# Seven-product blocks with additive weight sums, the first sum made by an accumulating DMA

## The chip, the cores and the metric

The kernel runs on one core of a Trainium2 chip. The metric is the device time of one execution in microseconds; the median of three runs of the kernel before is 1709.31 us (1709.23 to 1712.28). TensorE (PE) multiplies, VectorE (DVE) and ScalarE (ACT) work elementwise, GpSimd (POOL) and SyncE (SP) here mostly issue transfers; the program's DMAs run on 16 DMA engines.

## The reference

One decoder block on 256 tokens of width 2048, in float32: a SwiGLU FFN at half weight, a mixer of two head groups, a second FFN, and a final norm. The change touches the two FFNs alone.

```python
def swiglu_ffn(x, w_gate, w_up, w_down):
    return (jax.nn.silu(x @ w_gate) * (x @ w_up)) @ w_down
...
x = x + 0.5 * swiglu_ffn(rms_norm(x, ffn1_norm), ffn1_w_gate, ffn1_w_up, ffn1_w_down)
...
x = x + 0.5 * swiglu_ffn(rms_norm(x, ffn2_norm), ffn2_w_gate, ffn2_w_up, ffn2_w_down)
return rms_norm(x, final_norm)
```

The gate and up weights are 2048 x 5632, the down weights 5632 x 2048.

## The kernel before

**Units and splits.** Weights come in units of 512 x 512 (1 MB), as tiles `raw_...` of 128 partitions by 4 x 512. For accuracy every operand is taken as a high part and a low part: ACT casts the unit to its high part `hi` in two halves, VectorE subtracts to get the low part `lo`, and a product of a unit with 128 tokens is 12 matmuls of 128x512: eight with the high part, four with the low part. `parts_of` (line 180) does the split, `multiply` (line 231) the matmuls. Three sets of `hi` and `lo` are in use inside an FFN, so the splitting may run three units ahead of TensorE.

**A block of seven products.** `seven` (line 396) computes two token halves by two column groups of 512 for two of the row units with seven unit products in place of eight (Strassen's scheme in Winograd's form), and adds the other row units (`xs`) in the usual way. With four row units, as for gate and up, that is 7 x 12 + 4 x 24 = 180 matmuls. It uses four PSUM banks `a`, `c`, `e`, `d`. In the code's numbering, product 0 (p0) is w11, product 4 (p4) w12 - w11, product 5 (p5) w22 less that, product 6 (p6) w22 - w12, product 3 (p3) w21 less p5's operand, and products 2 and 1 are w22 and w21 by themselves. The differences are made on VectorE in the tiles of w11 and w12. p4 is copied out of bank `c` (`s5`) and added later; a product that serves two quadrants is copied out by ACT (`snap`). The stationary sides (`sf`) are sums of the normalised tokens, made once per FFN, or once per group of hidden units, by `seven_of` (line 360). Names in the trace carry these numbers: `lo_u1_2_p4` is the low part for p4 of block 2 of the first FFN's up projection, `x01` the first unit taken in the usual way.

**Order and queues.** Each FFN has five column steps `s`; each runs a gate block and an up block, and after steps 0, 2 and 4 the down projection `down`, with one block of its own and some plain units. That makes 13 blocks per FFN, 26 in all. All loads stand in one queue on SP, in the order of the program; each waits for its buffer. There are three `raw` buffers, and two `kept` ones for w11 and w12 of a block, which live through most of it: w12's is free after product 6's split, w11's after product 3's. The first block of the first FFN is special: its w11 is loaded and split ahead of it (`ready`). Within an engine instructions run in the order that the scheduler of the build gave them; the flag `order` pins a few.

Of the kernel before, what the change touches and what calls it, by code (L numbers as in the profile page):

```python
# [13 lines left out]
AF = mybir.ActivationFunctionType  # L14
ALU = mybir.AluOpType
AX = mybir.AxisListType

P = 128
# [6 lines left out]
CW = 512  # L25
NC_D = D // CW
UK = 4
# [22 lines left out]
def hybrid_block(ctx: ExitStack, tc: tile.TileContext, a: dict, out: bass.AP):  # L50
    nc = tc.nc
    Engine.pinned = False
    dve, act, pe = (Engine(tc, e) for e in (nc.vector, nc.scalar, nc.tensor))
# [105 lines left out]
    def load(src, name, pieces=((0, UK),), loaded=None, kept=False):  # L159
        if kept:  # L160
            raw = extra[1].tile([P, UK, CW], F32, tag="kept", name=f"raw_{name}", bufs=2)
        else:
            raw = raws.tile([P, UK, CW], F32, tag="raw", name=f"raw_{name}")
        for i, e in pieces:
            nc.sync.dma_start(raw[:, i:e, :], src[i * P : e * P].rearrange("(j p) c -> p j c", p=P))
            if loaded:
                loaded(i)
        return raw

    def splits_of(name):  # L170
        pool, bufs = splits, 2
        if extra:
            turn_of["split"] += 1
            if turn_of["split"] % 3 == 0:
                pool, bufs = extra[0], 1
        hi = pool.tile([P, UK, CW], F32R, tag="hi", name=f"hi_{name}", bufs=bufs)
        lo = pool.tile([P, UK, CW], F32R, tag="lo", name=f"lo_{name}", bufs=bufs)
        return hi, lo, [(hi[:, j, :], lo[:, j, :]) for j in range(UK)]
# [181 lines left out]
    def seven_of(sf, x0, x1, v, spare, parts, steps=None):  # L360

        a11, a12, a21, a22 = v[0, 0], v[0, 1], v[1, 0], v[1, 1]
        parts = iter(parts)

        def split(i, q):
            hi, lo = next(parts)
            act.copy(hi, q)
            dve.tensor_tensor(lo, q, f32(hi), op=ALU.subtract)  # L370
            sf[i] = [(hi[:, j, :], lo[:, j, :]) for j in range(UK)]

        sf.update({0: stationary(x0, 0), 1: stationary(x1, 0), 3: stationary(x1, 1)})
        dve.tensor_tensor(spare, a21, a22, op=ALU.add)
        split(4, spare)

        def adds():
            dve.tensor_tensor(a21, a11, a21, op=ALU.subtract)
            dve.tensor_tensor(a11, spare, a11, op=ALU.subtract)

        def rest():
            if steps is None:
                adds()
            split(5, a11)
            split(6, a21)
            dve.tensor_tensor(a12, a12, a11, op=ALU.subtract)
            split(2, a12)

        if steps is not None:
            steps.extend((adds, rest))  # L390
        return rest
# [1 line left out]
    def quad(tile):  # L393
        return tile.rearrange("p (j c) -> p j c", j=UK)

    def seven(w, rows, cols, sf, xs, name, keep, done, between=None, ready=None, whole=True, order=False):


        a, c, e, d = (bank(f"ps_{name}_{n}") for n in "aced")

        def get(u, n, kept=False):
            src = w[u * UK * P : (u + 1) * UK * P, cols[n] : cols[n] + CW]
            return load(src, f"{name}_{u}{n}", kept=kept)

        (r0, r1), two = rows, len(xs) > 1
        w11, first = ready or (get(r0, 0, True), None)
        w12 = get(r0, 1, True)
        b2, w22 = get(xs[0][0], 1), get(r1, 1)
        b3 = get(xs[1][0], 1) if two else None
        a2, w21 = get(xs[0][0], 0), get(r1, 0)  # L410
        a3 = get(xs[1][0], 0) if two else None

        def snap(ps, n):
            s = keep(f"{n}_{name}")
            act.copy(s, ps)
# [10 lines left out]
        product_of(0, w11, a, True, blk=first)  # L426
        s1 = None if whole else snap(a, "s1")
        if whole:
            act.copy(d, a)
        hi, lo, blk = splits_of(f"{name}_p4")  # L430
        for i in (0, 2):
            o = slice(i, i + 2)
            dve.tensor_tensor(w11[:, o], w12[:, o], w11[:, o], op=ALU.subtract)
            act.copy(hi[:, o], w11[:, o])
        for i in (0, 2):
            o = slice(i, i + 2)
            ins = dve.tensor_tensor(lo[:, o], w11[:, o], f32(hi[:, o]), op=ALU.subtract)
            if order:
                tc.keep_in_program_order(ins)
        product_of(4, w11, c, True, blk=blk)  # L440
        s5 = snap(c, "s5")
        if between:
            between(0)
        usual(0, b2, 1, (e, 1, True, not two), (c, 0, False, False))
        if between:
            between(1)
        dve.tensor_tensor(w11, w22, w11, op=ALU.subtract)
        product_of(5, w11, a)
        u2 = snap(a, "u2")
        if between:  # L450
            between(2)
        if two:
            usual(1, b3, 1, (e, 1, False, True), (c, 0, False, False))
        ins = dve.tensor_tensor(w12, w22, w12, op=ALU.subtract)
        if order:
            tc.keep_in_program_order(ins)
        product_of(6, w12, a)
        u3 = snap(a, "u3")
        done(1, 1, e, [u3, s5])
        product_of(2, w22, c)  # L460
        done(0, 1, c, [u2])
        usual(0, a2, 0, (d, 0, not whole, False), (a, 1, False, False))
        dve.tensor_tensor(w11, w21, w11, op=ALU.subtract)
        product_of(3, w11, a, end=not two)
        if two:
            usual(1, a3, 0, (a, 1, False, True), (d, 0, False, False))
        done(1, 0, a, [])
        product_of(1, w21, d)
        done(0, 0, d, [] if whole else [s1])

    def ffn(tag, norm, after, opening=False):
        with (
# [30 lines left out]
            units, vs, sf, ready = [], {}, {}, []  # L503
# [36 lines left out]
            ps = {(m, t): bank(f"ps_{m}{tag}_0_{t}") for m in "gu" for t in range(NT)}  # L540
# [182 lines left out]
            xs = list(enumerate(units))[2:]  # L723
# [77 lines left out]
            for s in range(5):  # L801
                cs = (CW + 2 * s * CW, 2 * CW + 2 * s * CW)
                sg = {}

                def total(ps, tiles):
                    for p in tiles[1:]:
                        dve.tensor_tensor(tiles[0], tiles[0], p, op=ALU.add)
                    if not tiles:
                        return ps
                    dve.tensor_tensor(tiles[0], ps, tiles[0], op=ALU.add)  # L810
                    return tiles[0]

# [12 lines left out]

                seven(wg, (0, 1), cs, sf, xs, f"g{tag}_{s}", keep, gate, meanwhile, ready.pop() if ready else None,
                      s > 0 and (tag, s) != (1, 3), s in (2, 4))
                seven(wu, (0, 1), cs, sf, xs, f"u{tag}_{s}", keep, up)
                if s % 2 == 0:
                    down(s == 4)  # L830
# [43 lines left out]
    with tc.tile_pool(name="mixer", bufs=1) as mp, tc.tile_pool(name="mixw", bufs=2) as mw:  # L874
# [208 lines left out]
        def row_factor(u):  # L1083
# [21 lines left out]
        for c, g in [(0, 0), (1, 0), (0, 1), (1, 1), (2, 0), (2, 1), (3, 0), (3, 1)]:  # L1105
# [3 lines left out]
            ps = product(w_out, c, (2 * g, 2 * g + 1), yT.__getitem__, f"o{c}_{g}", turn if (c, g) == (0, 1) else None)  # L1109
# [104 lines left out]
```

## Time and profile before

| | |
|---|---|
| median of three runs | 1709.31 us |
| the profiled execution, its own time | 1709.04 us |
| its span in the profile | 1707.3 us |
| mean granted TensorE clock | 0.999 |
| matmuls | 7471, busy 1690.1 us |
| DMA queue of SP | 360.75 MB, 66.3% of 16 engines' span |
| HBM read | 339.82 MB |

A row of a group reads: line, engine, operation, output and inputs by the program's names, shapes, count, then busy time and mean ns of one, then the engine's idle time ahead of them and what ended it. All engine instructions pass through one helper, so their line is L43; loads are L165. In the view of windows a row is a stretch in us from the span's start, its length, and each engine's busy time in it with the count of instructions, then the granted clock, the busy share of the DMA engines and GB/s. In a timeline the first two numbers are start and duration in us, of a run of like instructions.

### The profile page before, as it was taken

The numbers are of one execution on the slowest core, as the hardware profiler recorded it, in microseconds if no ns is written. First come the engines' busy times: TensorE is split into PE (matmuls) and PEld (weight loads), VectorE is DVE, ScalarE is ACT, GpSimd is POOL, SyncE is SP. The second block draws the span as 40 slices with busy tenths as digits, with TensorE's granted clock in tenths as the row PEclk, the third lists the DMA queues.
The fourth block names the chain that finished last, engine by engine and source line by source line (L and its number), as shares of the span: only waits on it lengthen the run. The fifth ranks groups of instructions, "written<-read, shape, count | busy, mean of one in ns | idle before, by whom it ended". The sixth has DMA issues, their size and how long they took to land. (4 is left out here: it accounts for less than half of the span.)

```text
span 1707.3 us, 19494 instructions
## 1 busy us (share of the span) xinstructions
PE 1690.1 (99%) x7471; PEld 1394.7 (82%) x7471; DVE 1456.5 (85%) x1217; ACT 1206.9 (71%) x1501; POOL 6.3 (0%) x20
## 2 busy tenths in 40 slices
PE   8999999999999999999999999999999999999998
PEld 7888888888888888888888888888888888888886
DVE  7998988889889889668696679989989888889796
ACT  7867667776567678877877777685567765677764
POOL 1000000000000000000000000000000000000000
PEclk9999999999999999999999999999999999999999
DMA  8666567585567684875657694585666656576853
GB/s 307 205 230 197 197 222 222 182 276 189 191 202 206 233 270 131 258 216 191 213 190 221 191 301 161 198 271 185 222 213 205 220 188 222 197 216 203 248 196 123
DMA packets 254173, 363.11 MB, mean 213 GB/s; under 512 B 85892, under 2 KB 88320, under 8 KB 253952
## 3 DMA queue, kind: packets, MB, share of 16 engines
q1 hardware_dynamic: 253616, 360.75, 66.3%
q8 instruction: 58, 0.95, 0.2%
q10 hardware_dynamic: 144, 1.05, 0.2%
q14 instruction: 35, 0.29, 0.0%
q0 software_dynamic: 320, 0.07, 0.0%
HBM read 339.82 MB, written 2.10 MB: 200 GB/s over the span
## 5 line engine op out<-in xcount | busy, mean ns | idle before, releaser
L43 ACT CAST hi_u_p<-raw_u 128x1024 fp32r<-128x1024 f32 x140 | 141.5, 1047 | 56.8 <-DVE raw_u L43 27.1
L43 ACT CAST hi_g_p<-raw_g 128x1024 fp32r<-128x1024 f32 x132 | 134.0, 1047 | 57.8 <-DVE raw_g L43 26.1
L43 DVE TENSOR_TENSOR lo_u_p<-raw_u,hi_u_p 128x2048 fp32r<-128x2048 f32 (+1 forms) x80 | 160.0, 2019 | 14.7 <-ACT hi_u_p L43 14.2
L43 DVE TENSOR_TENSOR lo_g_p<-raw_g,hi_g_p 128x2048 fp32r<-128x2048 f32 (+1 forms) x75 | 151.7, 2031 | 20.4 <-ACT hi_g_p L43 19.7
L43 PE MATMUL ps_d<-hi_d,h 128*128 128x512 f32 x704 | 167.0, 389 | 0.0
L43 PEld LDWEIGHTS ps_d<-hi_d,h 128*128 128x128 f32 x704 | 132.1, 188 | 27.4
L43 PE MATMUL ps_in<-hi_in,xT_nm 128*128 128x512 f32 x640 | 151.9, 390 | 0.0
L43 PEld LDWEIGHTS ps_in<-hi_in,xT_nm 128*128 128x128 f32 x640 | 119.5, 188 | 24.6
L43 DVE TENSOR_TENSOR lo_in<-raw_in,hi_in 128x2048 fp32r<-128x2048 f32 x40 | 91.3, 2286 | 47.6 <-ACT hi_in L43 47.2
L43 ACT CAST hi_d_p<-raw_d 128x1024 fp32r<-128x1024 f32 x84 | 86.4, 1048 | 64.0 <-DVE raw_d L43 22.6
L43 DVE TENSOR_TENSOR lo_d<-raw_d,hi_d 128x2048 fp32r<-128x2048 f32 x44 | 100.2, 2288 | 34.0 <-ACT hi_d L43 33.9
L43 ACT CAST hi_u_x<-raw_u 128x1024 fp32r<-128x1024 f32 x80 | 81.2, 1047 | 38.6 <-PE ps_u_c L43 24.6
L43 DVE TENSOR_TENSOR lo_d_p<-raw_d,hi_d_p 128x2048 fp32r<-128x2048 f32 (+1 forms) x48 | 96.5, 2020 | 9.3 <-ACT hi_d_p L43 8.8
L43 ACT CAST hi_d<-raw_d 128x1024 fp32r<-128x1024 f32 x88 | 88.9, 1046 | 19.6 <-PE ps_d_d L43 7.6
L43 ACT CAST hi_in<-raw_in 128x1024 fp32r<-128x1024 f32 x80 | 80.8, 1046 | 30.3 <-PE ps_in L43 24.8
L43 DVE TENSOR_TENSOR raw_u<-raw_u,raw_u 128x2048 f32<-128x2048 f32 (+1 forms) x50 | 92.3, 1862 | 11.6 <-DMA raw_u<-in_ffn_w_up_dram 10.9
L43 DVE TENSOR_TENSOR lo_g_x<-raw_g,hi_g_x 128x2048 fp32r<-128x2048 f32 x40 | 91.4, 2285 | 9.2 <-ACT hi_g_x L43 9.1
L43 ACT CAST hi_g_x<-raw_g 128x1024 fp32r<-128x1024 f32 x80 | 81.2, 1046 | 22.3 <-PE ps_g_c L43 9.2
L43 DVE TENSOR_TENSOR lo_u_x<-raw_u,hi_u_x 128x2048 fp32r<-128x2048 f32 x40 | 91.4, 2284 | 1.3 <-ACT hi_u_x L43 1.1
L43 DVE TENSOR_TENSOR raw_g<-raw_g,raw_g 128x2048 f32<-128x2048 f32 (+1 forms) x46 | 84.9, 1868 | 4.7 <-DMA raw_g<-in_ffn_w_gate_dram 4.5
L43 PE MATMUL ps_d<-lo_d,h 128*128 128x512 f32 x352 | 87.3, 389 | 0.0
L43 PE MATMUL ps_in<-lo_in,xT_nm 128*128 128x512 f32 x320 | 79.0, 389 | 0.0
(402 smaller groups left out, 3661.4 us busy)
## 6 DMA issues: line engine op xcount, KB each, us to landing
raw_d<-in_ffn_w_down_dram SPq DMA_DIRECT2D x88, 1024.0 KB, 5.8
raw_u<-in_ffn_w_up_dram SPq DMA_DIRECT2D x87, 1024.0 KB, 5.3
raw_g<-in_ffn_w_gate_dram SPq DMA_DIRECT2D x86, 1024.0 KB, 5.3
raw_in<-in_w_in_dram SPq DMA_DIRECT2D x40, 1024.0 KB, 5.1
raw_o<-in_w_out_dram SPq DMA_DIRECT2D x16, 1024.0 KB, 5.9
xres<-in_x_dram SPq DMA_DIRECT2D x4, 512.0 KB, 7.6
raw_u<-in_ffn_w_up_dram SPq DMA_DIRECT2D x2, 512.0 KB, 9.3
raw_g_first<-in_ffn_w_gate_dram SPq DMA_DIRECT2D x1, 1024.0 KB, 12.0
```

The source lines that it names most:

```text
L43: ins = getattr(self.engine, name)(*args, **kwargs)
```

## The change

The weights are now combined by sums where they were differences, with signs moved to the token side and to the snapshots (`scale=sign`): p4's operand is w12 + w11, p5's is that plus w22, p3's that plus w21, and p6's is p5's operand less w11. So one tile, `run`, carries a running sum, and w11's own tile is needed unchanged until p6.

In the 25 blocks other than `ready`, `run` is loaded with w12 by SP, and then POOL issues a DMA that reads w11 from HBM and adds it to the tile in flight; w11 is loaded a second time, into its own tile, for p0. p4 is now the first product. In 24 of these blocks its result is not kept aside and added later: ACT copies bank `c` into bank `e`, and the matmuls of quadrant `e` add to it (`seeded`). The pins by `order` go.

```diff
-        dve.tensor_tensor(spare, a21, a22, op=ALU.add)
+        dve.tensor_tensor(spare, a21, a22, op=ALU.subtract)
...
-            dve.tensor_tensor(a12, a12, a11, op=ALU.subtract)
+            dve.tensor_tensor(a12, a12, a11, op=ALU.add)
...
         (r0, r1), two = rows, len(xs) > 1
-        w11, first = ready or (get(r0, 0, True), None)
-        w12 = get(r0, 1, True)
+        if ready:
+            w11, first = ready
+            run = get(r0, 1, True)
+        else:
+            run, first = get(r0, 1, True), None
+            nc.gpsimd.dma_start(run, of(r0, 0).rearrange("(j p) c -> p j c", p=P), accum_op=ALU.add)
+            w11 = get(r0, 0, True)
...
-        def snap(ps, n):
+        def snap(ps, n, sign=1.0):
             s = keep(f"{n}_{name}")
-            act.copy(s, ps)
+            act.activation(s, ps, AF.Copy, scale=sign)
             return s
...
+        def corner():
+            product_of(0, w11, a, True, blk=first)
+            if whole:
+                act.copy(d, a)
+                return []
+            return [snap(a, "s1")]
...
+        else:
+            product_of(4, run, c, True)
+            if seeded:
+                act.copy(e, c)
+            s5 = [] if seeded else [snap(c, "s5")]
+            s1 = corner()
...
-        usual(0, b2, 1, (e, 1, True, not two), (c, 0, False, False))
+        usual(0, b2, 1, (e, 1, not seeded, not two), (c, 0, False, False))
...
-        dve.tensor_tensor(w11, w22, w11, op=ALU.subtract)
-        product_of(5, w11, a)
-        u2 = snap(a, "u2")
+        dve.tensor_tensor(run, run, w22, op=ALU.add)
+        product_of(5, run, a)
+        u2 = snap(a, "u2", -1.0)
...
-        ins = dve.tensor_tensor(w12, w22, w12, op=ALU.subtract)
...
-        product_of(6, w12, a)
-        u3 = snap(a, "u3")
-        done(1, 1, e, [u3, s5])
+        dve.tensor_tensor(w11, run, w11, op=ALU.subtract)
+        product_of(6, w11, a)
+        u3 = snap(a, "u3", -1.0)
+        done(1, 1, e, [u3] + s5)
...
-        dve.tensor_tensor(w11, w21, w11, op=ALU.subtract)
-        product_of(3, w11, a, end=not two)
+        dve.tensor_tensor(run, run, w21, op=ALU.add)
+        product_of(3, run, a, end=not two)
...
-                      s > 0 and (tag, s) != (1, 3), s in (2, 4))
+                      s > 0 and (tag, s) != (1, 3), (tag, s) not in ((1, 0), (1, 3)))
```

The `ready` block keeps p0 first, then p4 with its sum in halves on VectorE, as before.

What this does to the instructions on VectorE, at the start of the up block of step 2 in the first FFN (`raw_u1_2_00` is w11, `_01` w12 and later the running sum, `_11` w22, `_10` w21). Before:

```order
L43 TENSOR_TENSOR lo_u1_2_p0_2447<-raw_u1_2_00_2430,hi_u1_2_p0_2446 128x2048
L43 TENSOR_TENSOR raw_u1_2_00_2430<-raw_u1_2_01_2432,raw_u1_2_00_2430 128x1024 x2
L43 TENSOR_TENSOR raw_u1_2_01_2432<-raw_u1_2_11_2436,raw_u1_2_01_2432 128x2048
L43 TENSOR_TENSOR lo_u1_2_p4_2465<-raw_u1_2_00_2430,hi_u1_2_p4_2464 128x1024 x2
L43 TENSOR_TENSOR lo_u1_2_x01_2487<-raw_u1_2_21_2434,hi_u1_2_x01_2486 128x2048
L43 TENSOR_TENSOR raw_u1_2_00_2430<-raw_u1_2_11_2436,raw_u1_2_00_2430 128x2048
L43 TENSOR_TENSOR lo_u1_2_p5_2517<-raw_u1_2_00_2430,hi_u1_2_p5_2516 128x2048
```

And of the changed kernel, at the same place:

```order
L43 TENSOR_TENSOR lo_u1_2_p4_2428<-raw_u1_2_01_2410,hi_u1_2_p4_2427 128x2048
L43 TENSOR_TENSOR raw_u1_2_01_2410<-raw_u1_2_01_2410,raw_u1_2_11_2417 128x2048
L43 TENSOR_TENSOR lo_u1_2_p0_2446<-raw_u1_2_00_2413,hi_u1_2_p0_2445 128x2048
L43 TENSOR_TENSOR raw_u1_2_00_2413<-raw_u1_2_01_2410,raw_u1_2_00_2413 128x2048
L43 TENSOR_TENSOR lo_u1_2_x01_2464<-raw_u1_2_21_2415,hi_u1_2_x01_2463 128x2048
L43 TENSOR_TENSOR lo_u1_2_p5_2494<-raw_u1_2_01_2410,hi_u1_2_p5_2493 128x2048
```

The two half differences ahead of p4 are gone, p4's low part is one instruction, and it stands first; the sum for p5 has moved ahead of p0's low part, and the difference for p6 ahead of x01's.

On SP, the queue of loads around the same block's start, before:

```order
L165 DMA raw_u1_2_00_2430<-in_ffn1_w_up_dram 128x4x512
L165 DMA raw_g1_2_30_2153<-in_ffn1_w_gate_dram 128x4x512
L165 DMA raw_u1_2_21_2434<-in_ffn1_w_up_dram 128x4x512
L165 DMA raw_u1_2_01_2432<-in_ffn1_w_up_dram 128x4x512
L165 DMA raw_u1_2_11_2436<-in_ffn1_w_up_dram 128x4x512
```

And after:

```order
L165 DMA raw_u1_2_01_2410<-in_ffn1_w_up_dram 128x4x512
L165 DMA raw_g1_2_30_2138<-in_ffn1_w_gate_dram 128x4x512
L165 DMA raw_u1_2_21_2415<-in_ffn1_w_up_dram 128x4x512
L165 DMA raw_u1_2_00_2413<-in_ffn1_w_up_dram 128x4x512
L165 DMA raw_u1_2_11_2417<-in_ffn1_w_up_dram 128x4x512
```

w12 and w11 have changed places: the tile of the running sum takes the early load, in the previous block, and w11 the later one. POOL's queue gets, for each of the 25 blocks, one row such as `L413 DMA raw_u1_2_01_2410<-in_ffn1_w_up_dram 128x4x512`.

On ACT, at the same place in the changed kernel (`z1_2` are results of the gate block that are still to be finished):

```order
L43 CAST hi_u1_2_p4_2427<-raw_u1_2_01_2410 128x1024 x2
L43 CAST hi_u1_2_p0_2445<-raw_u1_2_00_2413 128x1024
L43 ACTIVATE z1_2_2385<-ps_g1_2_a_2119 128x512
L43 CAST hi_u1_2_p0_2445<-raw_u1_2_00_2413 128x1024
L43 CAST hi_u1_2_x01_2463<-raw_u1_2_21_2415 128x1024
L43 ACTIVATE z1_2_2404<-ps_g1_2_d_2122 128x512
L43 CAST hi_u1_2_x01_2463<-raw_u1_2_21_2415 128x1024
L43 CAST hi_u1_2_p5_2493<-raw_u1_2_01_2410 128x1024
L43 COPY ps_u1_2_e_2408<-ps_u1_2_c_2407 128x512
```

The casts for p4 stand first and so wait for the sum; the copy of bank `c` into `e` stands behind the first cast for p5.

More of the change, by code (lines that the diff above doesn't have):

```diff
@@ L394, in quad, with seven, of @@
         return tile.rearrange("p (j c) -> p j c", j=UK)
-    def seven(w, rows, cols, sf, xs, name, keep, done, between=None, ready=None, whole=True, order=False):
+    def seven(w, rows, cols, sf, xs, name, keep, done, between=None, ready=None, whole=True, seeded=True):
         a, c, e, d = (bank(f"ps_{name}_{n}") for n in "aced")
+        def of(u, n):
+            return w[u * UK * P : (u + 1) * UK * P, cols[n] : cols[n] + CW]
         def get(u, n, kept=False):
-            src = w[u * UK * P : (u + 1) * UK * P, cols[n] : cols[n] + CW]
-            return load(src, f"{name}_{u}{n}", kept=kept)
+            return load(of(u, n), f"{name}_{u}{n}", kept=kept)
         (r0, r1), two = rows, len(xs) > 1
-        w11, first = ready or (get(r0, 0, True), None)
-        w12 = get(r0, 1, True)
+        if ready:
[5 more added lines that the diff above has]
+            w11 = get(r0, 0, True)
         b2, w22 = get(xs[0][0], 1), get(r1, 1)
@@ L424, in usual @@
             multiply([(ps, stationary(xs[i][1], t), b, z) for ps, t, b, z in targets], blk, True)
[L426 to L441, printed above, removed]
+        def corner():
[4 more added lines that the diff above has]
+            return [snap(a, "s1")]
+        if ready:
+            s1 = corner()
+            hi, lo, blk = splits_of(f"{name}_p4")
+            for i in (0, 2):
+                o = slice(i, i + 2)
+                dve.tensor_tensor(run[:, o], run[:, o], w11[:, o], op=ALU.add)
+                act.copy(hi[:, o], run[:, o])
+            for i in (0, 2):
+                o = slice(i, i + 2)
+                dve.tensor_tensor(lo[:, o], run[:, o], f32(hi[:, o]), op=ALU.subtract)
+            product_of(4, run, c, True, blk=blk)
+            s5 = [snap(c, "s5")]
+        else:
[3 more added lines that the diff above has]
+            s5 = [] if seeded else [snap(c, "s5")]
+            s1 = corner()
         if between:
             between(0)
-        usual(0, b2, 1, (e, 1, True, not two), (c, 0, False, False))
+        usual(0, b2, 1, (e, 1, not seeded, not two), (c, 0, False, False))
         if between:
             between(1)
-        dve.tensor_tensor(w11, w22, w11, op=ALU.subtract)
-        product_of(5, w11, a)
-        u2 = snap(a, "u2")
+        dve.tensor_tensor(run, run, w22, op=ALU.add)
+        product_of(5, run, a)
+        u2 = snap(a, "u2", -1.0)
         if between:
@@ L453, in seven @@
             usual(1, b3, 1, (e, 1, False, True), (c, 0, False, False))
-        ins = dve.tensor_tensor(w12, w22, w12, op=ALU.subtract)
-        if order:
-            tc.keep_in_program_order(ins)
-        product_of(6, w12, a)
-        u3 = snap(a, "u3")
-        done(1, 1, e, [u3, s5])
+        dve.tensor_tensor(w11, run, w11, op=ALU.subtract)
+        product_of(6, w11, a)
+        u3 = snap(a, "u3", -1.0)
+        done(1, 1, e, [u3] + s5)
         product_of(2, w22, c)
@@ L468, in seven @@
         product_of(1, w21, d)
-        done(0, 0, d, [] if whole else [s1])
+        done(0, 0, d, s1)
     def ffn(tag, norm, after, opening=False):
```

## The prediction, on record before the run

> **What bounds the kernel now.** First the page's busy shares.
>
> ```profile
> span 1707.3 us, 19494 instructions
> PE 1690.1 (99%) x7471; PEld 1394.7 (82%) x7471; DVE 1456.5 (85%) x1217; ACT 1206.9 (71%) x1501; POOL 6.3 (0%) x20
> ```
>
> TensorE is busy nearly all the span, but "busy" may hide waits, because the ends of its matmuls are modelled. So I took stretches of one block each (180 matmuls of 128x512, from the block's first matmul to the next one's), in the view of windows. The first row is a block that waits for nothing; the other fence holds the first and the last of the twelve blocks that are longer, and their sum.
>
> ```profile
> 241.26:282.06 40.80, 40.80 (x181) 33.78 (x180) 35.80 (x24) 27.42 (x31) 0.00 (x0) 1.00 0.68 219
> ```
>
> ```profile
> core 0: us, PE busy (x) PEld busy (x) DVE busy (x) ACT busy (x) POOL busy (x), PEclk, DMA share, GB/s
> 55.73:97.00 41.27, 41.27 (x181) 33.55 (x180) 40.52 (x26) 32.65 (x38) 0.00 (x0) 1.00 0.71 221
> 282.06:323.50 41.44, 41.09 (x181) 33.71 (x180) 38.57 (x26) 31.95 (x38) 0.00 (x0) 1.00 0.68 216
> ...
> 646.18:687.54 41.36, 41.11 (x181) 33.71 (x180) 35.88 (x36) 37.22 (x56) 0.00 (x0) 1.00 0.61 170
> ...
> 1097.14:1139.11 41.97, 41.33 (x182) 33.63 (x180) 37.41 (x25) 31.93 (x37) 0.00 (x0) 1.00 0.71 224
> ...
> 1531.93:1573.49 41.56, 41.13 (x182) 33.71 (x180) 39.84 (x26) 33.34 (x39) 0.00 (x0) 1.00 0.67 215
> sum 495.68, PE 493.16 PEld 404.43 DVE 448.40 ACT 373.14 POOL 0.00; mean PE 41.10 PEld 33.70 DVE 37.37 ACT 31.09 POOL 0.00
> ```
>
> 40.80 us for 180 matmuls at full granted clock is the pace of the array. The twelve together lose 495.68 - 12 x 40.80 = 6.1 us, and the other fourteen blocks nothing worth counting. The number of matmuls does not change, so **6.1 us (0.36%) is all that this change can win**; the start, the tail and the mixer are untouched. Where it is lost, the timelines of TensorE and VectorE show:
>
> ```profile
> 292.94 1.97 PE L43 MATMUL ps_g_a<-hi_g_p,xs 128*128 128x512 f32 x8
> 295.26 1.19 PE L43 MATMUL ps_g_a<-lo_g_p,xs 128*128 128x512 f32 x4 [0.35 <-DVE lo_g_p L43]
> ```
>
> ```profile
> 279.89 2.35 DVE L43 TENSOR_TENSOR raw_g<-raw_g,raw_g 128x1024 f32<-128x1024 f32 x2
> ...
> 290.32 2.28 DVE L43 TENSOR_TENSOR lo_g_x<-raw_g,hi_g_x 128x2048 fp32r<-128x2048 f32 x1
> 292.92 2.29 DVE L43 TENSOR_TENSOR lo_g_p<-raw_g,hi_g_p 128x2048 fp32r<-128x2048 f32 x1 [0.31 <-ACT hi_g_p L43]
> ```
>
> It is product 5's low part: VectorE comes to it late, after the differences of weights. In such a stretch VectorE is the engine behind TensorE.
>
> **The change, part by part.** VectorE, by shape:
>
> ```profile
> L43 DVE TENSOR_TENSOR lo_u_p<-raw_u,hi_u_p 128x2048 fp32r<-128x2048 f32 x60 | 136.2, 2285 | 14.7 <-ACT hi_u_p L43 14.2
> L43 DVE TENSOR_TENSOR lo_u_p<-raw_u,hi_u_p 128x1024 fp32r<-128x1024 f32 x20 | 23.8, 1219 | 0.0
> L43 DVE TENSOR_TENSOR raw_u<-raw_u,raw_u 128x1024 f32<-128x1024 f32 x20 | 23.6, 1222 | 3.0 <-DMA raw_u<-in_ffn_w_up_dram 2.7
> L43 DVE TENSOR_TENSOR u_g<-u_g,s_g 128x512 f32<-128x512 f32 x12 | 8.2, 686 | 1.8 <-ACT u_g L43 1.8
> ```
>
> *Removed:* in 25 of 26 blocks the two half differences for product 4 (2 x 1.22 us) go, and its low part becomes one instruction (2.29) for two (2.44): 2.6 us a block, 65 us in all. The seed spares the addition of product 4 in 24 blocks: 24 x 0.69 = 16 us. VectorE falls from 1456 to about 1375 us (81%). That is off the path but for the twelve waits. ACT keeps its count: the snapshot of product 4 becomes a copy into PSUM, the other snapshots are scaled copies of the same shape.
>
> Relief by stage: 2.6 us before product 5 is more than the wait there, 0.6 to 0.8 us in four gate blocks (2.7 together, of 282.06's kind) and 0.2 to 0.4 in three up blocks (1.0). Those I count as gone: 3.7 us. Of the block at 1097.14 (1.2 us, VectorE too) I count half, 0.6, since it has least room below; of the first block half of 0.47, as it keeps its own sum. The block at 646.18 waits beside a crowded ACT (37.22 us busy), which does not change: nothing. Sum: 3.7 + 0.6 + 0.2 = **4.5 us gained**, between 0 and 6.1.
>
> *Moved:* product 4 stands first, and the third unit (x01) now waits for ACT's copy of c into e. That copy starts when product 4's twelve matmuls end and has product 0's twelve as cover (2.7 us, 12/180 of 40.80) for about 0.6 us; cost nothing, unless ACT stands at a later cast, when it would be some tenths per block. VectorE's sum for product 5 now stands ahead of product 0's low part and waits for w22's load; behind it wait that low part and x01's.
>
> *Added:* one accumulating load per block, issued by POOL after the first load has landed, and the block's first cast behind it. On POOL only the later blocks' sums stand behind it; on ACT everything behind that cast waits too, with TensorE some eight us of split units ahead (315.67 against 323.50, below). No row shows such a load. Bounds from issue to landing:
>
> ```profile
> raw_u<-in_ffn_w_up_dram SPq DMA_DIRECT2D x87, 1024.0 KB, 5.3
> ...
> rows_first<-in_ffn_norm_dram SPq DMA_DIRECT2D x1, 8.0 KB, 1.7
> rows_many<-in_mix_norm_dram POOLq DMA_DIRECT2D x1, 8.0 KB, 4.8
> ```
>
> Data of 1 MB takes 5.3 - 1.7 = 3.6 us; POOL's path with almost no data 4.8. A plain load by POOL would so land in 8.4, and below 5.3 it cannot be. The accumulating one also reads the tile that it adds to, one more pass: 4.8 + 7.2 = 12.0. The upper bound is 4.8 + 2 x 7.2 = 19.2, when SP's loads take every second turn. That can be, by the windows ahead of three block starts, where the DMA engines are nearly full:
>
> ```profile
> 215.00:241.00 26.00, 22.47 (x14) 1.00 0.80 281
> 302.00:323.00 21.00, 18.77 (x13) 1.00 0.85 293
> 1077.00:1097.00 20.00, 17.34 (x13) 1.00 0.85 308
> ```
>
> I take 12.0, nearest to the rows as they stand. [...]
>
> How late may it land? SP's issue of the block's first load, and TensorE's first matmul of that block:
>
> ```profile
> 215.66 0.37 SPq L165 DMA_DIRECT2D raw_u<-in_ffn_w_up_dram  x1
> 302.74 0.37 SPq L165 DMA_DIRECT2D raw_u<-in_ffn_w_up_dram  x1
> 340.82 0.37 SPq L165 DMA_DIRECT2D raw_d<-in_ffn_w_down_dram  x1
> 1077.11 0.37 SPq L165 DMA_DIRECT2D raw_u<-in_ffn_w_up_dram  x1
> ```
>
> ```profile
> 241.26 1.98 PE L43 MATMUL ps_u_a<-hi_u_p,x 128*128 128x512 f32 x8
> 323.50 1.98 PE L43 MATMUL ps_u_a<-hi_u_p,x 128*128 128x512 f32 x8
> 397.71 0.50 PE L43 MATMUL ps_d_a<-hi_d_p,h 128*128 128x512 f32 x1
> 1097.14 1.98 PE L43 MATMUL ps_u_a<-hi_u_p,x 128*128 128x512 f32 x8
> ```
>
> ```profile
> 315.67 1.99 ACT L43 CAST hi_u_p<-raw_u 128x1024 fp32r<-128x1024 f32 x2
> ```
>
> The order shows that the sum's tile gets the buffer and the place in SP's queue that w11 had, so these times hold for it. After the sum has landed come two casts (1.99) and three VectorE instructions (low part 4, sum 5, low part 0; 3 x 2.29): 8.9 us. The last is wanted 20 matmuls (4.5 us) after the block's first. So the sum must land 4.3 us before the first matmul. With a load of 5.3 us, 9.6 us of the time between the two rows are taken, and the rest is room for the sum: 16.0 at 241.26 (25.6 - 9.6), 11.2 at 323.50, 10.4 at 1097.14, 47.3 at 397.71. Read so over all 25 blocks, nine have 27 us or more (those of the down product, and those some way behind one); eleven have 13.2 to 17.6; five, like 323.50 and 1097.14, have 10.4 to 11.5. In those five the buffer comes free with product 6's low part, which VectorE makes late in the same late stretch as above; 2.6 us saved there make them 13.0 to 14.1. **At 12.0 us nothing waits**, with one microsecond to spare at the closest place.
>
> Total: 1709.04 (the profiled execution's own) - 4.5 = 1704.5; the median of the runs shown is 0.27 above that execution, so 1704.8.
>
> **Rivals.** *The sum lands late, and TensorE waits at the block's start* (slower). It decides from about 14.5 us: the overruns of the sixteen blocks then eat the 4.5. At 15 they add to 8 us (1712.8 with the gain taken off), at 16.5 to 20 (1725), at 19.2 to 58 (1763). For it: the 0.80 to 0.85 above, since the sum would take 7.2 us of engines that have 3 to 5 free in such a stretch, and would push the loads of w11 and w22 back too. Against it: the windows of whole blocks have 0.67 to 0.74, so the queue drains within the block, and SP's loads stay unissued while buffers are full.
>
> [...] I give it 0.05 of the chance below. [...]
>
> [...]
>
> *The five tight blocks do not move* (no change). The saved VectorE time is swallowed by ACT or by buffers; then at 12.0 they overrun by 4.1 us, nearly the gain: 1709. *The sum costs nothing and the gain does not come either*, since product 5's high part waits on ACT (the row at 292.92 names it): 1707 to 1709.
>
> **How the numbers follow.** Sum in time, gain taken: 0.44 (1702.9 to 1706.5). The two washes: 0.20 (1706 to 1712). Late: 0.36, a third of it below 1720, a third to 1735, a third above. Measurement of this kernel tells about 0.2% (3.4 us, so 1705.9 and 1712.7) from no change. Faster: 0.44, a little of it lost to 1706 and a little won from the washes. Range: from 1702.8 (all 6.1 gained) to 1732, which leaves out about 0.14 above and 0.04 below. The likeliest case's own range is 1702.9 to 1706.5.
>
> **What would show it.** Right: block windows of 40.80 us at 282, 531, 1283 and 1532; VectorE near 1375 us; DMA issue rows of POOL at 10 to 13 us to landing; no wait of ps_c for hi_p. Wrong: TensorE idle at the first product of up and gate blocks, "ACT hi <- DMA raw" long in the waits, landings of 15 us or more, or SP's own loads grown well beyond 5.3. If the gate blocks stay at 41.44 with the sum in time, VectorE was not the cause.

## The result, and the profile after

The changed kernel takes 1802.1 us (median of four runs, 1801.6 to 1805.5) against 1709.3 us for the kernel before on the same chip: a ratio of 1.0542, interval 1.0524 to 1.0561, so 5.4% slower. The prediction had 1704.8 us, range 1702.8 to 1732.0: wrong in sign, and outside its range.

The page of the kernel after: span, busy shares, DMA queues (packets, MB, share of 16 engines) and issues (KB each, median us from issue to landing).

```profile
span 1803.7 us, 19492 instructions
PE 1725.1 (96%) x7471; PEld 1405.2 (78%) x7471; DVE 1380.5 (77%) x1118; ACT 1204.4 (67%) x1501; POOL 38.8 (2%) x45
...
q1 hardware_dynamic: 253616, 360.75, 62.1%
q0 software_dynamic: 13520, 26.29, 8.4%
...
raw_d<-in_ffn_w_down_dram SPq DMA_DIRECT2D x88, 1024.0 KB, 6.1
raw_u<-in_ffn_w_up_dram SPq DMA_DIRECT2D x87, 1024.0 KB, 7.0
raw_g<-in_ffn_w_gate_dram SPq DMA_DIRECT2D x86, 1024.0 KB, 6.3
...
raw_u<-in_ffn_w_up_dram POOLq DMA_DIRECT2D x10, 1024.0 KB, 11.6
raw_g<-in_ffn_w_gate_dram POOLq DMA_DIRECT2D x9, 1024.0 KB, 12.9
raw_d<-in_ffn_w_down_dram POOLq DMA_DIRECT2D x6, 1024.0 KB, 12.6
```

VectorE is at 1380 us and the accumulating load lands in about 12 us, both as predicted. The 96 us of the span are elsewhere. TensorE's 7471 matmuls take 35 us longer (1725.1 against 1690.1), the other 61 us it stands. SP's loads of the up weights have grown from 5.3 to 7.0 us, and a median hides the worst: of the loads of FFN weights by SP, taken one by one from the issue rows, the 93 that were in flight together with an accumulating one took 10.1 (up), 10.9 (gate) and 10.6 us (down, medians), the other 174 took 5.3 to 5.6 (before: 5.3 to 5.8). Where that happens, windows show: from the issue of an up block's first load to its first matmul, and then that block and the gate block after it (the column before the last is the DMA engines' share; it counts the whole time of every packet that starts in the stretch, and so can pass 1).

```profile
226.52:251.49 24.97, 24.97 (x111) 20.65 (x111) 17.01 (x10) 14.06 (x17) 1.29 (x1) 1.00 1.01 318
```

```profile
251.49:297.73 46.24, 43.09 (x181) 34.61 (x180) 33.31 (x19) 27.27 (x31) 1.28 (x1) 0.96 0.68 194
297.73:340.48 42.75, 41.10 (x182) 33.71 (x180) 36.46 (x22) 32.33 (x38) 1.29 (x1) 1.00 0.83 250
```

The same stretch of the kernel before (215:241, in the prediction) had a DMA share of 0.80; now it is full from end to end. The block behind it takes 46.24 us instead of 40.80, though TensorE loses nothing inside the full stretch. It loses later, as timelines of this block show, VectorE first (in brackets idle time ahead of an instruction and what ended it).

```profile
249.09 2.29 DVE L43 TENSOR_TENSOR lo_u_p<-raw_u,hi_u_p 128x2048 fp32r<-128x2048 f32 x1 [5.73 <-ACT hi_u_p L43]
251.42 2.29 DVE L43 TENSOR_TENSOR raw_u<-raw_u,raw_u 128x2048 f32<-128x2048 f32 x1
253.63 2.28 DVE L43 TENSOR_TENSOR lo_u_p<-raw_u,hi_u_p 128x2048 fp32r<-128x2048 f32 x1
255.94 2.29 DVE L43 TENSOR_TENSOR raw_u<-raw_u,raw_u 128x2048 f32<-128x2048 f32 x1
258.15 2.28 DVE L43 TENSOR_TENSOR lo_u_x<-raw_u,hi_u_x 128x2048 fp32r<-128x2048 f32 x1
...
270.28 2.29 DVE L43 TENSOR_TENSOR raw_u<-raw_u,raw_u 128x2048 f32<-128x2048 f32 x1 [3.23 <-DMA raw_u<-in_ffn_w_up_dram]
272.49 2.28 DVE L43 TENSOR_TENSOR lo_u_p<-raw_u,hi_u_p 128x2048 fp32r<-128x2048 f32 x1
```

```profile
274.80 0.37 SPq L165 DMA_DIRECT2D raw_u<-in_ffn_w_up_dram  x1
```

```profile
285.74 1.04 ACT L43 CAST hi_u_x<-raw_u 128x1024 fp32r<-128x1024 f32 x1 [10.57 <-DMA raw_u<-in_ffn_w_up_dram]
```

```profile
286.83 1.20 PE L43 MATMUL ps_u_a<-hi_u_x,x 128*128 128x512 f32 x4 [2.45 <-ACT hi_u_x L43]
288.73 1.61 PE L43 MATMUL ps_u_a<-hi_u_x,x 128*128 128x512 f32 x4 [0.70 <-ACT hi_u_x L43]
290.14 3.19 PE L43 MATMUL ps_u_d<-hi_u_x,x 128*128 128x512 f32 x8
...
294.99 1.98 PE L43 MATMUL ps_u_d<-hi_u_p,x 128*128 128x512 f32 x8
```

The rows in turn: product 4's low part, which follows the accumulated sum (249.09; the sum's load was issued at 233.97 and took 13.0 us); the sum with w22 (251.42), whose load took 10.1 us and landed only 1.1 us ahead of the block (before: 5.7 us, landed 6.0 ahead); behind it product 0's low part (253.63), the difference for product 6 and x01's low part, which ends 8.9 us into the block, where before it ended 4.7 us in. TensorE does not yet wait, but x01's low part frees the buffer of SP's next load, and the low parts behind it those of the loads after that: these loads are issued some 4 us later than before, w21's 13.4 us into the block (before: 9.6). So w21 comes late, VectorE stands 3.2 us at the sum with it (270.28), and product 2's low part is queued behind, although that needs nothing that is late. Its end (274.77) frees the buffer for the block's last unit; SP issues that load 0.03 us later, 23.3 us into the block (before: 19.5). By now the next block's accumulating load is under way, and this one too takes 10.8 us. ACT waits 10.57 us for it, TensorE 2.45 and 0.70.

And then the array is slow: eight matmuls take 3.19 us, a little later 1.98. In between the granted clock (third column from the end) is halved:

```profile
289.30:292.70 3.40, 3.40 (x9) 2.62 (x8) 2.30 (x2) 2.46 (x3) 0.00 (x0) 0.50 0.92 224
```

Before its end the whole trace has eleven such stretches, of 3.4 or 6.8 us, each behind 3.4 us in which TensorE stood for 1.6 to 2.7 us; the kernel before has none. In the whole trace 168 matmuls start 0.3 to 0.5 us after the one before them, instead of 0.227; before there were 35. That is most of the 35 us by which the same matmuls take longer. Ahead of the stretch shown TensorE stood twice, 2.45 and 0.70 us; how long a stand it takes the runs do not show.

The view of waits, summed over the whole kernel (us, times, longest), first of the kernel after, then of before:

```profile
ACT hi_u_x L43 <- DMA raw_u<-in_ffn_w_up_dram: 60.3, 9, 10.9
ACT pair L43 <- DMA u_g<-pair: 42.7, 14, 6.3
...
DVE raw_u L43 <- DMA raw_u<-in_ffn_w_up_dram: 40.6, 18, 3.2
DVE raw_g L43 <- DMA raw_g<-in_ffn_w_gate_dram: 14.3, 11, 3.4
```

```profile
ACT hi_u_x L43 <- DMA raw_u<-in_ffn_w_up_dram: 11.2, 9, 1.9
ACT pair L43 <- DMA u_g<-pair: 8.1, 10, 1.8
...
DVE raw_u L43 <- DMA raw_u<-in_ffn_w_up_dram: 10.9, 10, 2.7
DVE raw_g L43 <- DMA raw_g<-in_ffn_w_gate_dram: 4.5, 4, 1.7
```

`pair <- DMA u_g` is ACT standing at the copies behind the transposing DMAs. In these rows both engines that feed TensorE stand three to five times as long before late transfers.

### The profile page after: what moved, and what is told of

It is laid out like the page before. It is cut to its first block, busy times and chain, and to the rows that moved or that the text cites. A ratio compares the mean times of both kernels' runs of the same rounds, so it can differ in the third digit from the quotient of the medians.

```text
span 1803.7 us, 19492 instructions
## 1 busy us (share of the span) xinstructions
PE 1725.1 (96%) x7471; PEld 1405.2 (78%) x7471; DVE 1380.5 (77%) x1118; ACT 1204.4 (67%) x1501; POOL 38.8 (2%) x45
## 3 DMA queue, kind: packets, MB, share of 16 engines
q0 software_dynamic: 13520, 26.29, 8.4%
## 4 chain that ended last, share of the span: by engine, by line
PE 64%; DMA 15%; DVE 9%; ACT 6%; issue 5%; SPq 0%; DVEq 0%; ACTq 0%
PE ps_in L43 11%; PE ps_d L43 10%; PE ps_g_a L43 6%; DMA raw_u<-in_ffn_w_up_dram 5%; PE ps_g_c L43 5%; PE ps_u_c L43 4%; DMA raw_g<-in_ffn_w_gate_dram 4%; DMA u_g<-pair 4%; PE ps_o L43 4%; PE ps_d_a L43 3%; PE ps_g_e L43 3%; PE ps_g_d L43 3%; PE ps_u_e L43 3%; PE ps_u_a L43 3%; PE ps_d_c L43 3%
## 5 line engine op out<-in xcount | busy, mean ns | idle before, releaser
L43 DVE TENSOR_TENSOR lo_u_p<-raw_u,hi_u_p 128x2048 fp32r<-128x2048 f32 x70 | 160.0, 2286 | 34.3 <-ACT hi_u_p L43 33.6
L43 PE MATMUL ps_d<-hi_d,h 128*128 128x512 f32 x704 | 172.0, 397 | 1.9 <-ACT hi_d L43 1.9
L43 ACT CAST hi_g_x<-raw_g 128x1024 fp32r<-128x1024 f32 x80 | 80.6, 1044 | 49.3 <-PE ps_g_c L43 17.8
L43 DVE TENSOR_TENSOR raw_u<-raw_u,raw_u 128x2048 f32<-128x2048 f32 x30 | 68.7, 2291 | 40.9 <-DMA raw_u<-in_ffn_w_up_dram 40.6
L43 DVE TENSOR_TENSOR lo_d_p<-raw_d,hi_d_p 128x2048 fp32r<-128x2048 f32 x42 | 95.8, 2285 | 4.9 <-ACT hi_d_p L43 4.8
L43 DVE TENSOR_TENSOR h<-pair,h 128x512 fp32r<-128x512 f32 x44 | 30.3, 689 | 71.5 <-ACT h L43 71.3
## 6 DMA issues: line engine op xcount, KB each, us to landing
raw_u<-in_ffn_w_up_dram POOLq DMA_DIRECT2D x10, 1024.0 KB, 11.6
raw_g<-in_ffn_w_gate_dram POOLq DMA_DIRECT2D x9, 1024.0 KB, 12.9
```

Source lines behind the costliest of these rows:

```text
L43: ins = getattr(self.engine, name)(*args, **kwargs)
```

## The experiments

Ratios are to the kernel before, run beside each group on the same chip (medians of 1708.7 to 1709.0 us). Only `seven` is changed (and a buffer in HBM declared where one is named).

**e1_dve_sum**: no accumulating load; VectorE makes the first sum.

```diff
-            nc.gpsimd.dma_start(run, of(r0, 0).rearrange("(j p) c -> p j c", p=P), accum_op=ALU.add)
             w11 = get(r0, 0, True)
...
+            dve.tensor_tensor(run, run, w11, op=ALU.add)
             product_of(4, run, c, True)
```

> The changed kernel without the accumulating load: w12 and w11 are loaded as before and VectorE makes the first sum (one instruction of 128x2048, some 2.29 us a block), with product 4 still first, the sums additive and the quadrant seeded. Three theories for the 93 us. LATE: the sum comes some 18 us after the block's first load is issued, the block's splits run later against TensorE, buffers come free later and the loads that wait for them miss their use. TRAFFIC: the extra 1 MB per block slows the other transfers. SEED: product 4 ahead of product 0 and the copy into e put new waits into the block. LATE and TRAFFIC expect 1703 to 1712 us here, since the sum needs only two loads and 2.3 us; SEED expects 1770 us or more.

Measured: 1724.4 us, ratio 1.0091 (1.0073 to 1.0109). 78 of the 93 us are gone, but 15 remain, more than LATE or TRAFFIC allowed. The order of VectorE's and ACT's instructions also differs here, so this run alone decides little.

**e2_traffic**: e1_dve_sum with the accumulating traffic beside it, into HBM.

```diff
...
+            mark = nc.gpsimd.tensor_copy(aside[1], run[:, UK - 1, CW - 1 :])
+            with tc.issue_after(mark.ins):
+                nc.gpsimd.dma_start(aside[0], of(r0, 0), accum_op=ALU.add)
             w11 = get(r0, 0, True)
```

> The kernel of e1_dve_sum (sum on VectorE) and beside it the same accumulating load of w11, issued by POOL once the block's first load has landed, but into a buffer in HBM that nobody reads: traffic of the same size at the same time, and nothing waits for it (one 128x1 copy on POOL marks the time). TRAFFIC expects most of the 93 us, 1770 us or more, with loads by SP at 7 us or more (median) as in the changed kernel. LATE and SEED expect the time of e1_dve_sum within 8 us.

Measured: 1822.5 us, 1.0660 (1.0644 to 1.0676), 98 us over e1_dve_sum. TRAFFIC alone can cost all of it. In this kernel it has a road of its own, since the first sum waits for w11's load, which it slows; so e9_traffic repeats it in the changed kernel's order.

**e3_wait, e5_wait3, e6_wait1**: the wait without the traffic; two, three or one small accumulating transfers in a row.

```diff
-            nc.gpsimd.dma_start(run, of(r0, 0).rearrange("(j p) c -> p j c", p=P), accum_op=ALU.add)
+            few = run[:, UK - 1 :, CW - 32 :]
+            few_of = of(r0, 0)[(UK - 1) * P :, CW - 32 :].rearrange("(j p) c -> p j c", p=P)
+            for _ in range(2):
+                nc.gpsimd.dma_start(few, few_of, accum_op=ALU.add)
```

> The changed kernel with the accumulating load cut to a thirty-second of the columns of a quarter of the rows, made twice, one behind the other: the sum is left out but for that corner (added twice), so the product is not the reference's; every instruction of ACT, VectorE and TensorE stands where the changed kernel has it. The wait for two transfers by POOL remains (an estimate from the smallest transfers of the rows, 2 to 5 us each, so 5 to 10 us where the changed kernel has 12), the traffic goes. LATE expects a loss in proportion to the wait: 1740 to 1790 us if the two take 8 to 10 us, less if they take 5. TRAFFIC expects 1703 to 1712 us with SP's loads back at 5.3 to 5.8 us. SEED, or the changed order of instructions alone, expects 1790 us or more.

> As e3_wait, with three small accumulating transfers in a row instead of two (the sum is left out but for that corner, so the product is not the reference's); all other engines' instructions stand as in the changed kernel. Two took 7.9 us (median, from the first's issue to the second's landing), so three should take 11 to 12, the wait of the changed kernel (12.1), with next to none of its traffic. LATE expects a good part of the 93 us: 1740 us or more. TRAFFIC expects 1707 to 1715 us.

> As e3_wait, with one small accumulating transfer (sum left out but for a corner, so the product is not the reference's): the wait is 3 to 5 us and the traffic nearly nothing. It shows what the change could win at most, VectorE at some 1385 us and the sum all but free. The prediction's gain of 4.5 us expects 1703 to 1706 us; a gain that is not there expects 1707 to 1710 us.

Measured: e6_wait1 1706.5 us, 0.9986 (0.9977 to 0.9994); e3_wait 1708.2, 0.9995 (0.9985 to 1.0005), its two transfers taking 7.9 us (median); e5_wait3 1730.9, 1.0128 (1.0110 to 1.0147), its three taking 13.4 us (10.2 to 17.8). SEED, and the changed order by itself, fall: with every instruction of the other engines in its place e3_wait loses nothing. LATE is real but small: a wait somewhat longer than the changed kernel's costs 22 us, one of 8 us nothing.

**e4_plain, e8_half**: an ordinary load of 1 MB, and an accumulating one of 512 KB.

```diff
-            nc.gpsimd.dma_start(run, of(r0, 0).rearrange("(j p) c -> p j c", p=P), accum_op=ALU.add)
+            nc.gpsimd.dma_start(run, of(r0, 0).rearrange("(j p) c -> p j c", p=P))
```

```diff
-            nc.gpsimd.dma_start(run, of(r0, 0).rearrange("(j p) c -> p j c", p=P), accum_op=ALU.add)
+            half = of(r0, 0)[: UK // 2 * P].rearrange("(j p) c -> p j c", p=P)
+            nc.gpsimd.dma_start(run[:, : UK // 2], half, accum_op=ALU.add)
```

> The changed kernel with an ordinary load by POOL in place of the accumulating one (w11 lands over w12, the sum is left out, so the product is not the reference's); the order of instructions is the same on every engine. It prices the accumulation itself. If the second pass over the tile costs what the prediction took (3.6 us of the 12.0), the load lands in 8 to 9 us: LATE then expects about a third of the 93 us back, 1765 to 1780 us; TRAFFIC expects the same direction, as the engines are held for less. If the accumulation is free, both expect 1802 us within 8.

> The changed kernel with the accumulating load cut to two of four row groups (512 KB; the other half of the sum is left out, so the product is not the reference's); order of instructions as in the changed kernel. By the packets' time it should hold the 16 engines for about 3.0 us a block, as the ordinary load of 1 MB did (2.9). If engine time is the price, 1715 to 1735 us, like e4_plain's 1725; if the accumulation is dear in itself (latency of its passes, order behind it), 1750 us or more.

Measured: e4_plain 1725.2 us, 1.0083 (1.0061 to 1.0106), more than either theory gave back; e8_half 1719.9, 1.0064 (1.0050 to 1.0077). POOL's queue, first of e4_plain, then of e8_half:

```profile
q0 software_dynamic: 7120, 26.29, 4.2%
```

```profile
q0 software_dynamic: 7120, 13.18, 4.4%
```

Both hold the engines alike, 0.042 x 1715.5 / 25 = 2.9 us a block and 0.044 x 1715.3 / 25 = 3.0; the whole accumulating load 0.084 x 1803.7 / 25 = 6.1. An accumulated megabyte cost the engines here what two plain ones did, in packets too (13520 against 7120). Twice the engine time costs over five times the loss (93 against 11 and 16 us, of which the longer wait explains 22 at most): the loss does not grow in step with the traffic.

**e7_sbuf**: the addend from w11's tile in SBUF.

```diff
-            nc.gpsimd.dma_start(run, of(r0, 0).rearrange("(j p) c -> p j c", p=P), accum_op=ALU.add)
             w11 = get(r0, 0, True)
+            nc.gpsimd.dma_start(run, w11, accum_op=ALU.add)
```

> The changed kernel with the accumulating transfer taken from w11's own tile (loaded by SP just before) instead of from HBM: the second read of w11 from HBM goes, the passes over the tile in the DMA engines stay; the output is the reference's. If it is the work of the DMA engines that slows the others, 1790 to 1830 us and SP's loads beside it at 9 to 11 us; if it is HBM's rate, 1710 to 1750 us. The sum also waits for w11's landing, 1 to 2 us more.

Measured: 1861.7 us, 1.0885 (1.0837 to 1.0934), worse than expected: the transfer starts only when w11 has landed, 12.8 us ahead of the block's first matmul (median) against 23.4 in the changed kernel. So its time does not tell HBM and engines apart cleanly. Its transfers do in part: with no read from HBM the accumulation still takes 10.2 to 11.4 us to landing and SP's loads beside it 7.0, 8.6 and 10.0 (medians; alone 5.2 to 5.3).

**e9_traffic, e11_later**: e6_wait1 and, beside it, the full traffic into a buffer that nobody reads; once as early as in the changed kernel, once behind product 5's sum.

```diff
...
+            mark = nc.gpsimd.tensor_copy(aside[1], run[:, 0, :1])
+            with tc.issue_after(mark.ins):
+                nc.gpsimd.dma_start(aside[0], of(r0, 0), accum_op=ALU.add)
             w11 = get(r0, 0, True)
```

> The kernel of e6_wait1 (one small accumulating transfer; the sum left out but for a corner, so the product is not the reference's; order of instructions as in the changed kernel) and behind it, once the block's first load has landed, an accumulating load of 1 MB into a buffer in HBM that nobody reads. The wait for the sum is short, the traffic is the changed kernel's. TRAFFIC alone expects 1770 us or more. If traffic and lateness are needed together (each takes what is left of the other's room), it expects 1720 to 1760 us. LATE expects 1706 to 1712 us.

> As e9_traffic, with the same 1 MB of accumulating traffic issued later, once VectorE has made product 5's sum (some 6 to 9 us into the block) instead of some 15 us ahead of the block. If the stretch ahead of the block's start is what makes the traffic dear (its loads of w11 and w22 are late there), less than half the loss of e9_traffic remains; if any 6 us of the engines anywhere cost the same, e9_traffic's time within 15 us.

Measured: e9_traffic 1787.8 us, 1.0462 (1.0447 to 1.0477), 81 us over e6_wait1; e11_later 1715.0, 1.0036 (1.0022 to 1.0050), 9 us over it. The later transfer was issued at the block's first matmul, the earlier one 22 us ahead of it (medians of 25 blocks). The window ahead of the same up block, of e4_plain, e9_traffic and e11_later:

```profile
215.73:241.99 26.26, 26.26 (x117) 21.75 (x116) 21.14 (x11) 15.55 (x18) 0.76 (x1) 1.00 0.85 311
```

```profile
227.51:252.47 24.96, 24.96 (x111) 20.65 (x110) 18.30 (x10) 14.84 (x17) 4.09 (x3) 1.00 1.02 326
```

```profile
219.42:245.60 26.18, 26.18 (x117) 21.66 (x116) 21.17 (x11) 15.48 (x18) 2.11 (x3) 1.00 0.78 273
```

In this order of instructions it matters whether the stretch ahead of the block is full: with a share of 0.85 in it e4_plain loses 16 us (8 in the execution shown), with 1.02 e9_traffic loses 79, and the same traffic some 20 us later costs a tenth. The rows show one block; over the last 20 us ahead of each of the 26 blocks the median share is 0.76 in the kernel before, 0.86 in e4_plain, 0.93 in the changed kernel, 0.99 in e9_traffic and 0.75 in e11_later. That the traffic costs this time, and that its place in the block decides how much, is shown by e9_traffic and e11_later; the share at which it starts to cost was not measured more closely.

**e10_pin, e13_casts**: the changed kernel, its accumulating load untouched, with VectorE's two later sums kept behind the low parts that the program writes ahead of them; then also product 1's casts ahead of ACT's copies behind the transposes.

```diff
-        dve.tensor_tensor(run, run, w22, op=ALU.add)
+        tc.keep_in_program_order(dve.tensor_tensor(run, run, w22, op=ALU.add))
...
-        dve.tensor_tensor(run, run, w21, op=ALU.add)
+        tc.keep_in_program_order(dve.tensor_tensor(run, run, w21, op=ALU.add))
```

```diff
+        blk3 = parts_of(a3, f"{name}_x10") if two else None
+        blk1 = parts_of(w21, f"{name}_p1")
         if two:
-            usual(1, a3, 0, (a, 1, False, True), (d, 0, False, False))
+            multiply([(a, stationary(xs[1][1], 1), False, True), (d, stationary(xs[1][1], 0), False, False)], blk3, True)
...
-        product_of(1, w21, d)
+        product_of(1, w21, d, blk=blk1)
```

> The changed kernel with VectorE's two sums that read w22 and w21 kept where the program writes them, behind the low parts of product 0 and of the units x01 and x00, instead of ahead of them; the output is the reference's. In the changed kernel those low parts wait behind a sum that waits for a slow load. If standing in order behind the late loads is the road from traffic to TensorE, a good part comes back: 1750 to 1780 us. If the late loads hold up TensorE directly through their own casts, little does: 1790 to 1810 us.

> The kernel of e10_pin with product 1's casts written ahead of the unit x10's product, so that they stand on ACT ahead of the copies that wait for the transposing DMAs; the output is the reference's. TensorE waited 4.4 us for those casts and 7.7 us for the low parts behind them in e10_pin. If that is what is left of the order's part, 1725 to 1735 us; if the rest of the loss (34 us) comes from the wait for the sum itself and late loads, 1738 to 1745 us.

Measured: e10_pin 1742.8 us, 1.0199 (1.0172 to 1.0226); e13_casts 1725.9, 1.0100 (1.0084 to 1.0116). 59 us come back by where two instructions a block stand on VectorE, 17 more by two casts on ACT, with the DMA stretch as full as ever (the window ahead of the same block in e10_pin):

```profile
219.87:244.89 25.02, 24.13 (x106) 19.64 (x106) 18.44 (x10) 14.60 (x17) 1.29 (x1) 1.00 0.99 318
```

In e10_pin's waits VectorE no longer stands at a sum for a load at all.

**e14_pin_traffic, e15_pin_wait1**: e9_traffic and e6_wait1 in e10_pin's order.

> The kernel of e9_traffic (short wait, full traffic into a buffer in HBM that nobody reads; the sum left out but for a corner, so the product is not the reference's) with the two sums kept behind the low parts as in e10_pin. If standing in order behind the sums is the road by which the traffic costs 81 us there, little of it is left: 1710 to 1725 us. If the late loads reach TensorE by other ways, 1740 us or more.

> The base line for the two others: e6_wait1 (short wait, no traffic; the sum left out but for a corner, so the product is not the reference's) in the order of e10_pin. 1705 to 1710 us if the order itself costs nothing; what it takes beyond e6_wait1's 1706.5 is the price of the order.

Measured: e15_pin_wait1 1706.1 us, 0.9984 (0.9975 to 0.9993); e14_pin_traffic 1751.6, 1.0249 (1.0225 to 1.0274). The mended order costs nothing and takes the traffic's price from 81 to 46 us: a miss, 1710 to 1725 us had been expected. ACT stands at late transfers on its own (60 us behind the transposing DMAs, against 8.1 in the kernel before). The load into HBM is also somewhat heavier than the real one (12.3 to 13.8 us to landing in e9_traffic, against 11.6 to 12.9), so it may overstate.

**e12_dve_pin**: e1_dve_sum with the same two sums kept behind, a try for a version that beats both kernels.

> The kernel of e1_dve_sum (first sum by VectorE, no accumulating load; the output is the reference's) with the two later sums kept behind the low parts as in e10_pin. If e1_dve_sum's 15 us over the kernel before come from low parts that stand behind a sum that waits for its load, 1706 to 1711 us, a match for the kernel before and perhaps 1 to 3 us better, as VectorE has 20 us less to do; if they come from product 4's first sum waiting for w11, 1718 to 1726 us.

Measured: 1718.8 us, 1.0058 (1.0044 to 1.0072): 6 us better than e1_dve_sum, 10 worse than the kernel before, so most of e1_dve_sum's 15 us are not that order. No version was found that beats the kernel before; e15_pin_wait1, with the sum nearly free, shows that such a version could win 0.16%.

## Why the prediction was wrong

**The bound and the gain: right in three of four blocks, about half in sum.** With the sum nearly free (e6_wait1) the four gate blocks named in the prediction read:

```profile
282.22:323.02 40.80, 40.80 (x181) 33.78 (x180) 36.65 (x21) 32.35 (x38) 0.86 (x1) 1.00 0.67 220
530.24:571.71 41.47, 41.09 (x182) 33.71 (x180) 35.35 (x22) 32.88 (x38) 0.86 (x1) 1.00 0.67 216
1282.29:1323.09 40.80, 40.80 (x182) 33.78 (x180) 36.65 (x21) 32.36 (x38) 0.86 (x1) 1.00 0.67 220
1529.81:1570.61 40.80, 40.80 (x182) 33.78 (x180) 36.88 (x22) 32.36 (x38) 0.86 (x1) 1.00 0.67 220
```

Three of four are at 40.80. The medians gained 2.4 us (interval 1.0 to 3.9) and 2.6 in e15_pin_wait1, where 4.5 had been counted.

**Durations: right, the landing in part by luck.** VectorE 1380.5 us for 1375; landing 11.6 to 12.9 us for 12.0; engine time 6.1 us for the 7.2. But the 12.0 counted no crowding: the same megabyte added into HBM landed in 8.4 to 10.4 us in e11_later (medians), where there was room, and in 12.3 to 13.8 in e9_traffic. So the sum seems too long for a free path, and the crowding that it left out made up the rest. The one more pass that the prediction counted for the accumulating load shows in the engines' time: 6.1 us a block beside 2.9 for the plain load of e4_plain.

**"The sum must land 4.3 us before the first matmul": mostly met.** By the trace it landed so in 23 of 25 blocks (whose starts had themselves moved), and e5_wait3 prices the wait at 22 us or less. The room was cut too fine, not by much.

**What failed is the step "so the queue drains within the block".** The prediction had both numbers: 7.2 us of engines, with 3 to 5 free in the stretch ahead of a block. It set the overload aside by the whole block's share of 0.67 to 0.74, and reckoned every room with SP's loads at 5.3 us, so that their delay stood in its sum at nothing. The DMA engines do have room in a block, but in its first half, as the block at 251.49 of the changed kernel shows in two parts:

```profile
251.49:271.49 20.00, 20.00 (x89) 16.40 (x88) 16.73 (x8) 13.74 (x16) 0.00 (x0) 1.00 0.49 160
271.49:297.73 26.24, 23.09 (x93) 18.21 (x92) 16.58 (x12) 13.54 (x15) 1.28 (x1) 0.93 0.83 220
```

The room comes behind the full stretch, too late for the loads that are due in it: they took 10.1 to 10.9 us and arrived 5 us late, and a mean over 40 us says nothing of them. e9_traffic (early, 81 us) and e11_later (late, into that room, 9 us) show it. Of the signs that the prediction named for being wrong, these came: SP's own loads far beyond 5.3 us, and ACT long at loads; the landings stayed under 15 us but for one.

**And an order was named without a price.** "Behind it wait that low part and x01's", said the prediction of the sum with w22. It priced the wait of a sum at its own place in the order only, not the buffers that come free later behind it and the loads that are issued later for that. e10_pin puts that road at 59 of the 93 us, the slower matmuls behind stalls included; with the load into HBM in place of the real one it is 35 of 81 (e14_pin_traffic).

**The rivals.** The late sum had the right sign and, in half a sentence, the right cause (it "would push the loads of w11 and w22 back too"), but its price ran from the sum's landing alone, deciding at 14.5 us; the loss was there at 12. The copy into e behaved as said: next to free where ACT is on time (TensorE waited 0.4 us in all in e6_wait1), 13.7 us in the changed kernel, where it is not (8.9 in gate, 3.1 in up and 1.7 in down blocks). The 0.05 in the prediction is for a sum made late by POOL's own issue; no run shows that. In the changed kernel POOL's issuing instruction took 1.28 to 1.37 us in the 23 of 25 blocks where VectorE was busy all through it and 1.30 us in the one where VectorE stood still, and the sums landed after 12.1 us (median of the 23) and 13.4.

What stays open: whether the price of the traffic lies in the DMA engines' time or in HBM's rate, which e7_sbuf does not tell apart by its time; and how the 17 us left in e13_casts divide between the wait for the sum and transfers that are late in themselves.

## What to carry to other kernels

Weigh added traffic against the free share of DMA in the stretch where it will run, not against a mean over the whole loop: here 6 us did not fit into a stretch of 26 us that was 0.80 full, and cost a tenth as much some 20 us later (9 us against 81). Here a late transfer was mostly paid not by its own reader but behind it: look at what stands behind that reader on its engine (here product 2's low part, behind a sum for which VectorE stood 3.2 us), and which buffers that work frees. An instruction that waits for a load belongs behind work whose data are there: moving two sums so gave back 59 of the 93 us (e10_pin).

## What the runs showed of the hardware

An accumulating megabyte took the DMA engines 6.1 us where a plain one by the same queue took 2.9 (e4_plain), with about twice the packets (13520 against 7120 for the queue), and landed in 11.6 to 12.9 us where the plain one landed in 7.4 to 8.0 (medians, both beside other loads; into HBM, with more room, 8.4 to 10.4 in e11_later). With its addend in SBUF it took 10.2 to 11.4 us to landing (e7_sbuf). Loads by SP beside it took 10.1 to 10.9 us instead of 5.3 to 5.6; beside the plain one 7.6 to 8.0 (e4_plain).

In the changed kernel TensorE's stalls cost more than their length: of the 96 us of span, 61 are stalls and 35 the same matmuls taking longer. The lower clock accounts by estimate for some 27 of the 35 (mean granted clock 0.984 for 0.999, so 0.015 x 1803.7); where the other 8 come from is not shown. In e10_pin, whose stalls inside the blocks are 1.6 us at most, the clock is 0.998.
